# Which token blocks take the dense pass: the 4th, 5th and 8th in place of the 5th, 7th and 8th

## The chip, the cores and the metric

The kernel runs on one core of a Trainium2 chip. The metric is the device time of one execution in microseconds (us). The engines are named as the profile names them: PE (matrix products; PEld is its weight load), DVE (vector), ACT (scalar), POOL (GpSimd) and SP, whose queue issues most transfers.

## What is computed

One decoder layer over 1024 tokens of width 1024, in float32: a token mixer (stick-breaking attention and an mLSTM on one input projection, gated and projected), a layer norm, and then a mixture with 16384 experts, whose part matters here. Each of 8 heads picks 16 experts per token by the best sums of two sets of 128 keys:

```python
s1 = jnp.einsum('bshd,nd->bshn', q[..., 0, :], k1)
s2 = jnp.einsum('bshd,nd->bshn', q[..., 1, :], k2)
v1, i1 = lax.top_k(s1, 16); v2, i2 = lax.top_k(s2, 16)
...
top_s, pos = lax.top_k(cand, 16)
gates = jax.nn.softmax(top_s, axis=-1)
...
ue = jnp.take(u_tab, ib, axis=0)
act = jax.nn.gelu(jnp.einsum('btd,bthkd->bthk', hb, ue), approximate=False)
ve = jnp.take(v_tab, ib, axis=0)
return jnp.einsum('bthk,bthkd->btd', gb * act, ve)
```

The result of a token is this sum, plus a gated term of a per-layer embedding and the residual, through a last layer norm.

## The kernel before

The 1024 tokens are eight blocks of 128, worked on in three groups (`BLOCKS`): the 1st and 2nd; the 3rd, 4th and 5th; the 6th, 7th and 8th. The code counts blocks from 0, the text from 1. Each group goes through input projections, attention beside the mLSTM, branch projections, `keys` (the query projection and each head's best 16 keys), then `choose` (the best 16 sums and their experts, nearly all on DVE) beside `embed` (the rest of the layer's sum) and the next group's `project`.

A block's experts are worked out in one of two ways.

**Gathered.** Five blocks. `Experts` takes 128 rows of the table u and 128 rows of the table v (one for each of a token's 128 choices). POOL issues one indirect transfer for each row (`row`, L1079: 128 x 1024 floats into one of six buffers `vr`), and DVE multiplies and sums it: `vr<-vr,h1r` for u, `acc<-vr,w,acc` for v, both recorded at L139. The u rows of one block run alternately with the v rows of the block before it. Blocks are taken in the order in which they are chosen. This work lies in the background, between all else, from the first choice to the end.

**Dense.** Three blocks (`DENSE`). `dense` runs at the end over the whole tables in 128 pieces ("experts" in the loop over `e`): PE multiplies the tokens (`h1s`, 384 columns) with a piece of u (L276 to L278, into `m`), ACT applies gelu, DVE multiplies with the gates (`y<-y,gp`, L1043), and PE multiplies with the piece of v (L1019), accumulated in PSUM tiles `g` and `z`. There are two buffers `m`, so PE can be one piece ahead.

The gates come from a table in DRAM, `Gd`, which `spread` makes for each dense block, right after the block's `choose`. It transposes the choices (L965 to L967), and then works on 32 groups of four tokens. Of each group DVE makes one tile `ohA` (L977, 128 x 512), four one-hot rows `ohB` of 128 x 128 are made by the engines that `HOTS` names with a letter for each token (P is POOL, A is ACT with two instructions, D is DVE; L985 for P and D, L161 for A), PE multiplies (L987, four matmuls, into `z`, of which there are two), and ACT copies the product to `stage` (L173). After every four groups two transfers write `stage` to `Gd`. `ohA` and `ohB` come from one ring of `NCS` buffers (`csel`), and `stage` from the ring `c4` of four, which the attention's `kt` and `vt` use as well.

`ORDER` gives the order of the choices in the first two groups. In the third the dense blocks are chosen (and their tables made) beside `embed`, and the others beside the dense pass:

```python
h1s = halve()
yield from keys(o)
ex.rate = RATES["last"]
yield from Merge(choose(o, [t for t in o.tbs if t in DENSE]), embed(o))
ex.rate = RATES["dense"]
yield from Merge(choose(o, [t for t in o.tbs if t not in DENSE]), dense(h1s))
```

The order of the instructions on each engine is fixed when the program is built, by a scheduler that starts from this order of issue; each engine then runs its list in that order. The new names are `slot` (where a block's transposed tokens lie in `h1Ts`, by `OFF` and `SLOTS`) and `iota128`, the row that one-hot rows are compared with.

Of the kernel before, what the change touches and what calls it, by code (L numbers as in the profile page):

```python
# [20 lines left out]
P = 128  # L21
# [12 lines left out]
ORDER = [(0, 1), (2, 4, 3)]  # L34
# [3 lines left out]
NCS = 5  # L38
# [5 lines left out]
def _classes():  # L44
    """Where the n-th best of a head's sums can lie, n in fours: blocks of equal width, (to, from, a, b) each."""
    r, to = [], 0
    for lo in range(0, 16, 4):
        blocks = []
        for a0 in range(lo + 4):
            b0, b1 = lo // (a0 + 1), (lo + 4) // (a0 + 1)  # L50
            if b0 == b1:
                continue
            of, first, _, nb = [x for x in RANKS if x[1] <= a0 < x[2]][0]
            if blocks and blocks[-1][3] == a0 and blocks[-1][4:6] == (b0, b1) and blocks[-1][6] == (nb, first):
                blocks[-1] = blocks[-1][:3] + (a0 + 1,) + blocks[-1][4:]
            else:
                blocks.append((to, of + (a0 - first) * nb + b0, a0, a0 + 1, b0, b1, (nb, first)))
            to += b1 - b0
        r.append((blocks, to))
    return r  # L60
# [6 lines left out]
DENSE = (6, 7, 4)  # L67
OFF = (0, 128, 0)
HOTS = ("PAAD", "PAAD")
# [3 lines left out]
SLOTS = 4  # L73
# [7 lines left out]
class Merge:  # L81
    """Steps several emitters, always the one whose clock is furthest back."""
# [18 lines left out]
class Stream:  # L101
    """Streams the pieces of the weights in the order of their use, the loads and splits running ahead."""
# [17 lines left out]
def body(ctx: ExitStack, tc: tile.TileContext, a, out):  # L120
# [10 lines left out]
    class Chain:  # L131
        """The vector engine for work in the background, at most so many instructions in its queue at a time."""
# [15 lines left out]
    class Act:  # L148
        """The scalar engine: what needs one table set issues between two loads of sets."""
# [16 lines left out]
        def loose(self, o, i, f):  # L166
            """Out of that order: the set of the others is loaded again behind it."""
            x = nc.scalar.activation(o, i, f)
            if self.table not in (None, TABLES[f]):
                order(nc.scalar.preload_act_table_set(self.table), x)  # L170
# [100 lines left out]
    def mm(o, l, r, first, last):  # L271
        """One pass of plain float32 operands, or three of operands split in two."""
        if len(l) == 1:
            pe.matmul(o, l[0], r[0], start=first, stop=last)  # L274
        else:
            pe.matmul(o, l[0], r[0], start=first, stop=False)  # L276
            pe.matmul(o, l[0], r[1], start=False, stop=False)  # L277
            pe.matmul(o, l[1], r[0], start=False, stop=last)  # L278

    class Plain:  # L280
        """Operands of four slices each."""
# [12 lines left out]
    class Halves:  # L294
        """Two blocks of tokens, split in two."""
# [11 lines left out]
    def gemm(unit, other, blocks, evac, wide, width):  # L307
        """wide: the streamed weights are the moving operand, out = other^T @ w; else out = w^T @ other."""
# [29 lines left out]
    def standard(xt, st, read=None):  # L338
        """To mean 0 and variance 1, on the scalar engine; the sums of the halves may have been taken already."""
# [12 lines left out]
        # 1/sqrt by way of the logarithm, and a Newton step  # L352
# [10 lines left out]
    def layer_norm(xs, g, b):  # L363
        """In place, for as many blocks of tokens at a time as are given; one step for each."""
# [10 lines left out]
        # 1/sqrt: a first guess from the bits, good to 6%, then Newton steps to full precision  # L375
# [44 lines left out]
    # the order in which the weights are streamed  # L420
# [57 lines left out]
    def project(o):  # L478
        w, t0, hT = o.w, o.t0, o.hT
        rh = hT  # L480
        # gates of the recurrence, as rows
# [252 lines left out]
    def back(acc, hT, n, u, by, alone=False):  # L734
        """Adds a block's tokens, taken from their transposes, times the given diagonal."""
# [4 lines left out]
    def gates(o):  # L740
        """The attention's gates, but for the sigmoid."""
# [68 lines left out]
    def keys(o):  # L810
        w = o.w
        r1 = o.h1
        # the very first experts are wanted soon: the other block of tokens keeps its scores until they are chosen
# [59 lines left out]
    def choose(o, tbs):  # L873
        for tb in tbs:
# [48 lines left out]
            # a sum's place, in steps, plus its expert: the nearest to the place of the one that was taken  # L923
# [30 lines left out]
    def spread(tb, vidx, gt):  # L954
        """The gates of a block's tokens over all experts, to DRAM: per token a product of one-hot rows."""
# [7 lines left out]
        by = HOTS[tb in BLOCKS[-1]]  # L963
# [8 lines left out]
        for q in range(8):  # L972
            st = [c4("stage", (P, 64, 16)) for _ in range(2)]
            for t in range(q * 16, q * 16 + 16, 4):
# [4 lines left out]
                for k in range(4):  # L979
                    i2, gate, minus = (sel[:, i, t + k:t + k + 1] for i in (1, 2, 3))  # L980
                    if by[k] == "A":
                        act.activation(B[:, k], iota128, AF.Abs, bias=i2, scale=-1.0)
                        act.activation(B[:, k], B[:, k], AF.Relu, bias=gate, scale=minus)
                    else:
                        (pool if by[k] == "P" else vec).tensor_scalar(B[:, k], iota128, i2, gate, op0=OP.is_equal, op1=OP.mult)  # L985
# [14 lines left out]
    def halve():  # L1000
        """The dense blocks' tokens, split in two."""
# [7 lines left out]
    def dense(h1s):  # L1009
        """All experts' scores, times the gates, times the table v, accumulated in PSUM."""  # L1010
# [52 lines left out]
    class Experts:  # L1063
# [7 lines left out]
        def add(self, tb):  # L1071
            """For each block of tokens once its experts are chosen, and once the rest of its sum is stored."""
# [47 lines left out]
        def step(self):  # L1120
            """One slot; its time, or None when there is nothing to do."""
# [117 lines left out]
```

## Time and profile before

| | us |
|---|---|
| median of 3 runs (lowest to highest) | 3391.44 (3391.26 to 3399.57) |
| span of the profiled execution, first to last instruction | 3395.4 |
| PE busy | 3016.1 (89%) |
| DVE busy | 2652.0 (78%) |
| POOL busy | 1704.5 (50%) |
| ACT busy | 1108.9 (33%) |

The profile is of one execution. It shows its span, and no time outside it. Busy time is the time in which an engine has an instruction running; the chain that ended last follows the last instruction back through what released each step. The rows on which the prediction rests stand below, by view.

### The profile page before, as it was taken

How to read it: one execution, taken by the hardware profiler on the slowest of the kernel's cores; microseconds unless marked ns; L12 is line 12 of the kernel's file. 1: busy time of each engine (PE TensorE's matmuls, PEld its weight loads, DVE VectorE, ACT ScalarE, POOL GpSimd, SP SyncE). 2: the span in 40 equal slices, each digit the busy share in tenths (PEclk: the TensorE clock that was granted, in tenths of full speed). 3: DMA queues.
4: the chain of work that ended last, by engine and by line, in shares of the span. 5: the costliest groups of instructions: out<-in, count | busy, mean ns of one | idle time of the engine just before them, and what ended most of it. 6: DMA issues, size and time to landing. Idle time of an engine off the chain costs nothing.

```text
span 3395.4 us, 39154 instructions
## 1 busy us (share of the span) xinstructions
PE 3016.1 (89%) x12105; PEld 2024.1 (60%) x12105; DVE 2652.0 (78%) x5565; ACT 1108.9 (33%) x2561; POOL 1704.5 (50%) x1409
## 2 busy tenths in 40 slices
PE   7997999969899749998989664799999999999995
PEld 6876554555554535566555453566666666666663
DVE  5645998798699789888889977867777777776778
ACT  4626234521612445464141354411121111111110
POOL 0000255566533866646654577745545555544554
PEclk9898998969999859998999755799999999999997
DMA  6343798889989878977998776999999999999996
GB/s 212 130 155 136 246 351 324 318 276 378 357 307 319 323 267 308 339 263 251 376 358 320 272 266 229 311 344 351 354 361 349 345 348 350 350 353 357 352 343 244
DMA packets 341826, 1035.22 MB, mean 305 GB/s; under 512 B 38512, under 2 KB 95216, under 8 KB 341616
## 3 DMA queue, kind: packets, MB, share of 16 engines
q0 software_dynamic: 184320, 671.17, 55.2%
q1 hardware_dynamic: 157296, 361.55, 29.4%
q8 instruction: 96, 1.57, 0.2%
q14 instruction: 114, 0.93, 0.1%
HBM read 991.17 MB, written 41.42 MB: 304 GB/s over the span
## 4 chain that ended last, share of the span: by engine, by line
PE 69%; DVE 12%; issue 7%; POOL 5%; ACT 4%; DMA 2%; SPq 0%; DVEq 0%; POOLq 0%; ACTq 0%
PE g L274 17%; PE g L1019 13%; PE z L1019 6%; PE m L278 5%; PE m L276 5%; PE m L277 5%; PE g L784 3%; POOL ohB L985 3%; PE m L622 3%; POOL vr L1079 2%; PE z L987 2%; DVE vr L139 2%; PE z L583 2%; PE g L278 2%; PE g L276 2%
## 5 line engine op out<-in xcount | busy, mean ns | idle before, releaser
L1079 POOL DMA_INDIRECT vr<-in_u_dram,vidx x640 | 765.5, 1196 | 996.5 <-DVE V L139 385.8
L1079 POOL DMA_INDIRECT vr<-in_v_dram,vidx x640 | 793.2, 1239 | 648.5 <-DVE acc L139 333.9
L139 DVE SCALAR_TENSOR_TENSOR acc<-vr,w,acc 128x1024 f32<-128x1024 f32 x640 | 820.3, 1282 | 50.1 <-DMA vr<-in_v_dram,vidx 40.7
L139 DVE SCALAR_TENSOR_TENSOR vr<-vr,h1r 128x1024 f32<-128x1024 f32 x640 | 779.4, 1218 | 49.3 <-DMA vr<-in_u_dram,vidx 37.4
L1019 PE MATMUL g<-wf,y 128*128 128x512 f32 x1024 | 460.6, 592 | 1.6 <-DVE y L1043 1.6
L251 DVE TENSOR_TENSOR hl<-wf,hl 128x512 fp32r<-128x512 f32 x256 | 179.0, 699 | 306.3 <-PE m L277 268.7
L161 ACT ACTIVATE hl<-wf 128x512 fp32r<-128x512 f32 x256 | 160.5, 628 | 767.6 <-PE m L278 590.1
L276 PE MATMUL m<-h1s,hl 128*128 128x384 f32 x1024 | 395.3, 386 | 4.8 <-ACT y L161 3.1
L274 PE MATMUL g<-hT,wf 128*128 128x384 f32 x1024 | 344.1, 491 | 4.8 <-DVE gs L851 3.2
L278 PE MATMUL m<-h1s,hl 128*128 128x384 f32 x1024 | 345.8, 338 | 1.5 <-DVE hl L251 1.5
L277 PE MATMUL m<-h1s,hl 128*128 128x384 f32 x1024 | 345.4, 337 | 0.0
L1019 PEld LDWEIGHTS g<-wf,y 128*128 128x128 f32 x1024 | 192.2, 189 | 186.6 <-issue 169.7
L274 PEld LDWEIGHTS g<-hT,wf 128*128 128x128 f32 x1024 | 192.0, 191 | 135.1 <-issue 8.4
L987 PE MATMUL z<-ohA,ohB 128*128 128x128 f32 x768 | 182.7, 410 | 99.8 <-POOL ohB L985 90.5
L1019 PE MATMUL z<-wf,y 128*128 128x512 f32 x512 | 240.6, 592 | 0.0
L987 PEld LDWEIGHTS z<-ohA,ohB 128*128 128x128 f32 x768 | 155.7, 299 | 128.8 <-POOL ohB L985 115.4
L276 PEld LDWEIGHTS m<-h1s,hl 128*128 128x128 f32 x1024 | 193.8, 189 | 35.5 <-issue 31.3
L277 PEld LDWEIGHTS m<-h1s,hl 128*128 128x128 f32 x1024 | 193.8, 189 | 29.9 <-issue 29.9
L278 PEld LDWEIGHTS m<-h1s,hl 128*128 128x128 f32 x1024 | 193.4, 189 | 2.1 <-DVE hl L251 1.8
L274 PE MATMUL g<-h1T,wf 128*128 128x384 f32 x512 | 172.3, 491 | 0.1
L1019 PEld LDWEIGHTS z<-wf,y 128*128 128x128 f32 x512 | 97.3, 190 | 122.5 <-issue 122.2
L622 PE MATMUL m<-awT,vt 128*64 128x128 f32 x992 | 149.9, 302 | 18.7 <-ACT awT L173 12.1
(333 smaller groups left out, 4544.2 us busy)
## 6 DMA issues: line engine op xcount, KB each, us to landing
wf<-in_uE_dram SPq DMA_DIRECT2D x128, 512.0 KB
wf<-in_v_dram SPq DMA_DIRECT2D x128, 512.0 KB
wf<-in_wmain_dram SPq DMA_DIRECT2D x84, 512.0 KB
wf<-in_wgate_dram SPq DMA_DIRECT2D x48, 512.0 KB
wf<-in_wq_dram SPq DMA_DIRECT2D x48, 512.0 KB
Gd<-stage SPq DMA_DIRECT2D x48, 512.0 KB
gp<-Gd SPq DMA_DIRECT2D x32, 768.0 KB
wf<-in_wout_dram SPq DMA_DIRECT2D x24, 512.0 KB
```

What stands on the lines that cost most here:

```text
L139: x = getattr(vec, op)(*args, **kw)
L161: x = nc.scalar.activation(o, i, f, **kw)
L251: vec.tensor_tensor(lo, src, hi, op=OP.subtract)
L274: pe.matmul(o, l[0], r[0], start=first, stop=last)
L276: pe.matmul(o, l[0], r[0], start=first, stop=False)
L277: pe.matmul(o, l[0], r[1], start=False, stop=False)
L278: pe.matmul(o, l[1], r[0], start=False, stop=last)
L622: pe.matmul(po[rows, :P], vt[:, lo + s, row["e"] * 64:(row["e"] + 1) * 64], wT[:, s * P:(s + 1) * P], start=i == 0, stop=i == row["nb"] - 1)
L784: pe.matmul(acc, yT[k // 4][:, k % 4, n * P:(n + 1) * P], wo[u][k // 2][:, k % 2, :], start=k == 0, stop=k == 7)
L987: pe.matmul(pg[:, k], B[:, k], A[:, k], start=True, stop=True)
L1019: pe.matmul(acc[d][c], y[:, d * P:(d + 1) * P], wv[:, c * 512:(c + 1) * 512], start=e == 0, stop=e == P - 1)
L1079: pool.indirect_dma_start(out=vr, out_offset=None, in_=use[0], in_offset=bass.IndirectOffsetOnAxis(ap=idx[:, s:s + 1], axis=0))
```

## The change

The dense blocks become the 4th, 5th and 8th; gathered are the 1st, 2nd, 3rd, 6th and 7th. The second group chooses in the order 3rd, 4th, 5th, so that the tables of the 4th and 5th are made in that group's last stage, and the third group has one table to make and two choices beside the dense pass. POOL makes no one-hot rows: of each four, two are DVE's. The ring `csel` has 7 buffers for 5, there is room for five blocks of transposed tokens, since the 4th and the 5th must outlast the third group's writes, and the program is built with `dynamic_dma_scratch_size=8192`, which was not given before. Docstrings and comments went; the line numbers are the same.

```diff
-ORDER = [(0, 1), (2, 4, 3)]
+ORDER = [(0, 1), (2, 3, 4)]
...
-NCS = 5
+NCS = 7
...
-DENSE = (6, 7, 4)
-OFF = (0, 128, 0)
-HOTS = ("PAAD", "PAAD")
+DENSE = (3, 4, 7)
+OFF = (0, 256, 0)
+HOTS = "DAAD"
...
-SLOTS = 4
+SLOTS = 5
...
-        by = HOTS[tb in BLOCKS[-1]]
+        by = HOTS
...
-                        (pool if by[k] == "P" else vec).tensor_scalar(B[:, k], iota128, i2, gate, op0=OP.is_equal, op1=OP.mult)
+                        vec.tensor_scalar(B[:, k], iota128, i2, gate, op0=OP.is_equal, op1=OP.mult)
...
-    nc = bacc.Bacc("TRN2", target_bir_lowering=False, num_devices=1)
+    nc = bacc.Bacc("TRN2", target_bir_lowering=False, num_devices=1, dynamic_dma_scratch_size=8192)
```

How the lists of the engines change is shown at three places.

PE, from the second group's last projections (L274) to the first product of the third group's attention (L583); a piece of the difference, - is before:

```order
-L274 MATMUL g<-hT,wf 128x384 x4
+L274 MATMUL g<-hT,wf 128x384 x9
+L987 MATMUL z<-ohA,ohB 128x128 x8
+L274 MATMUL g<-hT,wf 128x384 x7
 L987 MATMUL z<-ohA,ohB 128x128 x104
+L965 MATMUL z<-ident,self 128x128
+L966 MATMUL z<-ident,self 128x128
+L967 MATMUL z<-ident,gt 128x128
+L987 MATMUL z<-ohA,ohB 128x128 x128
 L583 MATMUL z<-kt,qT 128x256
```

Of a table's 128 products 24 stand between projections, before as after; 104 follow the last of them, and now the whole table of the 5th block too, all ahead of the attention. In the third group one of two tables has gone from PE's list in the same way.

DVE, at the start of the dense pass of the changed kernel, between the gate products (L1043) of the third piece and those of the fourth; a cut from the middle of it:

```order
L1043 TENSOR_TENSOR y<-y,gp 128x192
L139 TENSOR_TENSOR ci<-top 128x8 x3
L139 TENSOR_TENSOR ci<-top 128x8x2
L251 TENSOR_TENSOR hl<-wf,hl 128x512
L139 CAST top<-pos 128x128
L139 TENSOR_TENSOR ci<-top 128x8x4
L139 SCALAR_TENSOR_TENSOR acc<-vr,w,acc 128x1024
L139 TENSOR_TENSOR ci<-top 128x8x2
L139 TENSOR_SCALAR top<-top 128x128
```

The `ci`, `top` and `pos` are the choice of the 6th block, and that of the 7th follows. Before the fourth piece's gate products stand 12 gathered rows of v and the end of one choice with the start of the next. From the last table's last `ohA` to the gate products of the seventh piece DVE's list holds 28 gathered rows and nearly two choices; before it held 21 and one.

DVE at the end, from the last piece's gate products to the statistics of the last layer norm, before:

```order
L1043 TENSOR_TENSOR y<-y,gp 128x192 x2
L139 SCALAR_TENSOR_TENSOR acc<-vr,w,acc 128x1024 x4
L1056 TENSOR_TENSOR accd<-accd,g 128x512 x2
L139 SCALAR_TENSOR_TENSOR acc<-vr,w,acc 128x1024
L1056 TENSOR_TENSOR accd<-accd,g 128x512 x2
L1056 TENSOR_TENSOR accd<-accd,z 128x512
L139 SCALAR_TENSOR_TENSOR acc<-vr,w,acc 128x1024
L1056 TENSOR_TENSOR accd<-accd,z 128x512
L139 SCALAR_TENSOR_TENSOR acc<-vr,w,acc 128x1024 x12
L370 BN_STATS st<-acc 128x6 x2
```

And of the change:

```order
L1043 TENSOR_TENSOR y<-y,gp 128x192 x2
L139 SCALAR_TENSOR_TENSOR acc<-vr,w,acc 128x1024 x4
L1056 TENSOR_TENSOR accd<-accd,g 128x512 x2
L139 SCALAR_TENSOR_TENSOR acc<-vr,w,acc 128x1024
L1056 TENSOR_TENSOR accd<-accd,g 128x512 x2
L139 SCALAR_TENSOR_TENSOR acc<-vr,w,acc 128x1024
L1056 TENSOR_TENSOR accd<-accd,z 128x512 x2
L139 SCALAR_TENSOR_TENSOR acc<-vr,w,acc 128x1024 x43
L370 BN_STATS st<-acc 128x6 x2
```

Behind the last gate products 18 gathered rows stood before, and now 49. Of the 1280 gathered rows 503 stood behind the first gate product of the dense pass, and now 544.

## Rows read from the trace of the kernel before

**Rows 1.** The page: chain that ended last, share of the span by engine.
```profile
PE 69%; DVE 12%; issue 7%; POOL 5%; ACT 4%; DMA 2%; SPq 0%; DVEq 0%; POOLq 0%; ACTq 0%
```

**Rows 2.** Busy time by stretch: length, busy us (instructions), granted clock, DMA share, GB/s.
```profile
1120.00:1226.00 106.00, 74.41 (x322) 58.07 (x320) 78.94 (x130) 60.87 (x185) 93.16 (x71) 0.77 0.83 294
1226.00:1257.00 31.00, 0.34 (x2) 0.34 (x2) 30.97 (x133) 5.12 (x7) 13.29 (x12) 0.50 0.81 283
1257.00:1925.00 668.00, 608.29 (x2405) 370.08 (x2404) 599.80 (x1279) 264.98 (x582) 373.29 (x311) 0.93 0.87 313
1925.00:2026.00 101.00, 66.59 (x259) 55.58 (x259) 71.02 (x128) 64.45 (x195) 86.53 (x65) 0.55 0.72 242
2026.00:2069.00 43.00, 0.88 (x3) 0.51 (x3) 42.48 (x141) 6.07 (x13) 25.48 (x20) 0.50 0.74 252
2069.00:2163.00 94.00, 63.93 (x259) 54.91 (x260) 65.67 (x118) 62.32 (x186) 81.60 (x62) 0.57 0.75 251
2163.00:3345.00 1182.00, 1177.28 (x4540) 813.26 (x4539) 859.34 (x1323) 211.21 (x383) 618.58 (x486) 1.00 0.96 349
```

**Rows 3.** PE in order of time, 5th block's table: start, us, what, [idle before].
```profile
1124.20 1.95 PE L987 MATMUL z<-ohA,ohB 128*128 128x128 f32 x16
...
1222.28 3.75 PE L987 MATMUL z<-ohA,ohB 128*128 128x128 f32 x16 [1.75 <-issue]
1256.69 1.19 PE L583 MATMUL z<-kt,qT 64*128 64x256 f32 x2 [30.66 <-DMA kt<-kTd]
```

**Rows 4.** PE in order of time, the tables of the 7th and 8th blocks.
```profile
1925.76 0.47 PE L965 MATMUL z<-ident,self 128*128 128x128 f32 x1 [7.20 <-DVE self L962]
...
1930.42 3.92 PE L987 MATMUL z<-ohA,ohB 128*128 128x128 f32 x16 [3.76 <-POOL ohB L985]
...
2024.04 1.09 PE L987 MATMUL z<-ohA,ohB 128*128 128x128 f32 x6 [0.34 <-ACT ohB L161]
2062.74 0.45 PE L965 MATMUL z<-ident,self 128*128 128x128 f32 x1 [37.61 <-DVE self L962]
...
2069.24 5.27 PE L987 MATMUL z<-ohA,ohB 128*128 128x128 f32 x24 [5.62 <-POOL ohB L985]
...
2160.39 2.08 PE L987 MATMUL z<-ohA,ohB 128*128 128x128 f32 x8 [2.00 <-POOL ohB L985]
```

**Rows 5.** Groups of instructions from 1925 to 2163 us: busy, mean ns, idle before.
```profile
L987 PE MATMUL z<-ohA,ohB 128*128 128x128 f32 x512 | 129.1, 427 | 68.2 <-POOL ohB L985 61.9 <-ACT ohB L161 5.5 <-ACT stage L173 0.4
...
L985 POOL TENSOR_SCALAR ohB<-iota,sel 128x128 f32<-128x128 f32 x64 | 97.5, 1524 | 15.0 <-PE z L987 12.8 <-issue 0.6 <-POOL ohB L985 0.2
...
L1079 POOL DMA_INDIRECT vr<-in_u_dram,vidx x41 | 49.1, 1197 | 14.5 <-issue 4.7 <-DVE top L139 2.6 <-DVE ci L139 1.7
...
L977 DVE TENSOR_TENSOR ohA<-iota,sel 128x512 f32<-128x512 f32 x64 | 43.8, 685 | 0.0
```

**Rows 6.** The same view over the whole span.
```profile
L1079 POOL DMA_INDIRECT vr<-in_u_dram,vidx x640 | 765.5, 1196 | 996.5 <-DVE V L139 385.8 <-DVE vr L139 283.0 <-issue 94.3
...
L985 DVE TENSOR_SCALAR ohB<-iota,sel 128x128 f32<-128x128 f32 x96 | 35.5, 370 | 74.9 <-PE z L987 72.5 <-issue 2.0
```

**Rows 7.** ACT in order of time, two groups of four tokens of the 8th block.
```profile
2123.19 0.66 ACT L173 ACTIVATE stage<-z 128x256 f32<-128x256 f32 x2 [1.73 <-PE z L987]
...
2125.59 1.64 ACT L161 ACTIVATE ohB<-ohB,sel 128x128 f32<-128x128 f32 x4
```

**Rows 8.** DVE in order of time: gate products of the sixth and seventh pieces.
```profile
2208.48 0.62 DVE L1043 TENSOR_TENSOR y<-y,gp 128x192 f32<-128x192 f32 x2
...
2216.68 0.63 DVE L1043 TENSOR_TENSOR y<-y,gp 128x192 f32<-128x192 f32 x2
```

**Rows 9.** DVE in order of time, from the last gate products to the end.
```profile
3343.98 0.62 DVE L1043 TENSOR_TENSOR y<-y,gp 128x192 f32<-128x192 f32 x2
3344.60 1.28 DVE L139 SCALAR_TENSOR_TENSOR acc<-vr,w,acc 128x1024 f32<-128x1024 f32 x1
...
3352.60 1.28 DVE L1056 TENSOR_TENSOR accd<-accd,g 128x512 f32<-128x512 f32 x2
...
3373.38 1.29 DVE L370 BATCH_NORM_STATS2 st<-acc 128x6 f32<-128x512 f32 x2
...
3387.26 3.67 DVE L387 SCALAR_TENSOR_TENSOR accd<-accd,rs,ln2b 128x1024 f32<-128x1024 f32 x3
```

## Prediction

> **What bounds the kernel now.** I read the chain of waits first: PE has 69% of it, DVE 12%, POOL 5% [rows 1]. So most of the time is PE's own work, which the change leaves alone: the same three blocks' worth of dense pass, the same projections. Then busy time by stretch [rows 2]. In the dense pass PE is busy for 1177.3 of 1182 us; nothing but PE counts there. In the three stretches in which a gate table is made PE's busy share falls to about two thirds at a granted clock of 0.55 to 0.77, and in the two in which a block is chosen with nothing beside it (1226 to 1257, 2026 to 2069) PE does next to nothing and DVE is busy throughout. These are the stretches that the change moves and shortens. In the tables POOL is busy for 87 of 101 and 82 of 94 us. The groups of instructions there say who is waited for: of PE's 68.2 us of idle time before L987, 61.9 ended with POOL's one-hot row, of 1524 ns each [rows 5]. So a table is bound by POOL, which makes one row of each four tokens between the gathers that it issues as well (1197 ns each).
>
> All sums are made against the profiled execution, whose span is 3395.4 us. No time around it is shown; it lies 4.0 us above the median of the three runs and within their range, so I take the difference off the median.
>
> **A group of four tokens.** Before, the 7th block's table took from 1930.42 to 2025.13 us, 94.7 us or 2.96 us for each of 32 groups; the 8th's took from 2069.24 to 2162.47, 2.91 [rows 4]. Without POOL, three engines are left:
> - ACT's work per group is unchanged: two groups ran from 2123.19 to 2127.23, 2.02 us each [rows 7].
> - PE: the first 24 records of the 8th's table are three groups (a product has two records: 512 records for 256 products), 5.27 us back to back at the lower clock, 1.76 each [rows 4].
> - DVE: one `ohA`, 0.685 us [rows 5], and now two `ohB` of 0.37 [rows 6], so 1.43, and with the gathered rows that its list holds between them. A row is 1.28 us [rows 9]. In the changed tables of the 5th and 8th blocks the list has about one row for two groups: 1.43 + 0.64 = 2.07. In the 4th's it has 30 for 32 groups.
>
> The unknown is how well these three interleave. The floor is ACT's 2.02, the ceiling 2.96, where nothing would be gained. I take **2.15**, near the floor, since two more one-hot buffers let DVE and ACT run further ahead of PE than before. A table is then 69 us.
>
> **The last stage of the second group (term A).** The 5th block's table began at 1124.20 and ended at 1226.03, 101.8 us, with the last projections between its first 24 products [rows 3]. The 4th block's takes its place. DVE's list is 32 x 1.43 + 30 x 1.28 = 84 us; as durations of neighbours overlap a little I take 80: -22. Behind it one choice and the attention followed: 1226.03 to 1256.69, 30.7 us. Now PE's list has the choice of the 5th, its table, and only then the attention. A choice up to the transposes it feeds took 2025.13 to 2062.74, 37.6 us [rows 4]; from the transposes to the first product 6.5 (2062.74 to 2069.24); the table 69; and `kt`, which waited last for its transfer at 1256.69 [rows 3], now gets its buffer from the table's last `stage` tiles: 2. That is 115.1 for 30.7, +84. **A = +62.** Only the 24 products stand beside projections; the second table is exposed.
>
> **The last stage of the third group (term B).** From the 7th block's transposes to the last product of the 8th's table: 1925.76 to 2162.47, 236.7 us [rows 4]. One choice and one table leave it. Left are 4.7 us from transposes to first product (1925.76 to 1930.42) and 69. **B = -163.**
>
> **The start of the dense pass (term C).** Two choices, not one, now stand beside the first pieces. From the last `ohA` to the seventh piece's gate products DVE's list has 7 rows more (9.0 us) and nearly one choice. A choice's own work is the 37.6 us less the 16 rows that its list holds (20.5): 17.1. So DVE is 26 us later at that point. Before, those products began at 2216.68, 8.2 us after the sixth's [rows 8], and the pace from there to the last, at 3343.98 [rows 9], is 9.32 us a piece over 121 pieces, PE's. PE can be one piece ahead, which covers about 9. **C = +17**, between 0 (two pieces ahead) and +33 (12 rows and one choice before the fourth piece's products, nothing covered).
>
> **The end (term D).** 49 rows instead of 18 stand behind the last gate products. Before, these 18 rows and six additions of 0.64 us took from 3344.60 to 3373.38; 24.9 us for 18 rows, 1.38 each [rows 9]. No PE work hides this. 31 x 1.38: **D = +43**. Bounds: 1.28, DVE alone (40), and the 2.43 of the dense pass, 1182 us for 486 rows with the tables' transfers beside them (75); the tail itself is the nearest.
>
> **At nothing.** Attention, branches and keys of the third group hold as many gathered rows as before to within two. POOL has 96 one-hot rows less, 142 us of work; outside the tables it waited mostly for DVE, for choices or for a buffer [rows 6], so this buys nothing by itself. The setting of `dynamic_dma_scratch_size` bears on POOL's transfers, and no row shows how: should it double the time that POOL lost to issue, 94.3 us for 640 gathers [rows 6], 0.15 each, the 49 last rows would cost 7 us more. The copies of the residual move from the 4th block to the 7th, two on ACT, which has 60% of that stage idle.
>
> **Sum.** 62 - 163 + 17 + 43 = **-41 us**; 3391.4 - 41 = **3350 us**.
>
> One rule of the skill speaks against the change. In the stretch 1925 to 2163 us POOL's gather took 1197 ns beside 64 one-hot rows of DVE, against 1196 over the whole span [rows 5, 6]: no hold is seen. The Trainium skill (SBUF — State Buffer, "Who interferes with whom") states that VectorE and GpSimd share a pair of ports, that VectorE's `tensor_scalar` may take both of it, and that the other then waits for the whole instruction, descriptor writing included. The trace's equal means don't bear that out for these operands. What it would cost is the third rival.
>
> **Rivals.**
> 1. *DVE takes POOL's place, slower than before.* DVE runs its list in order; a gathered row that is late holds the `ohA` and `ohB` behind it. If groups stay at 2.96 us, the three tables lose 22 + 2 x 26 = 74 us of what I gave them: +33, 3424 us. It decides from 2.60 us a group. For it: the 4th's DVE list alone is 84 us, and DVE was busy for 79 of 106 us there [rows 2]. Against it: PE waited for POOL, not DVE, and POOL now issues gathers without one-hot rows between them.
> 2. *The dense pass starts badly.* The two choices are chains of small instructions; if nothing is covered and the second choice holds the pieces behind as well (another 7 rows and 10 us), C is 52: -6, 3385 us, no change.
> 3. *The added one-hot rows hold the gathers.* 96 of them on DVE at 0.37 us, each holding one gather for its whole time and each seen on the path: +36, so -5, 3386 us, no change.
> 4. *Better than forecast.* Groups at ACT's 2.02, the 4th's table at 70, nothing lost at the start: -41 - 8 - 10 - 17 = -76, 3315 us.
>
> **How the numbers follow.** The forecast gets 0.65, the rivals 0.13, 0.11, 0.03 and 0.08. About 0.3% (10 us) is what a measurement of this kernel can tell from no change. Faster: the forecast, the fourth rival and a part of the second, 0.77. Same: most of the second and the third, 0.10. Slower: the first, 0.13. The forecast's own bounds are 8 us either way for the two tables, 10 for the 4th's, 17 for C, and 3 below to 15 above for D. The range reaches up over the second and third rivals to the edge of no change and down nearly to the fourth: 3318 to 3395.
>
> **What would show it.** Three tables of 65 to 75, 65 to 75 and 75 to 90 us between first and last L987; the third attention's first L583 at 1310 to 1330 us; the dense pass ending about 85 us earlier than 3344; 49 gathered rows behind it at 1.3 to 1.5 us. A group of more than 2.6 us, or PE idle for more than 40 us in the first seven pieces, makes the prediction wrong.

## The result, and the profile after

| | before | after |
|---|---|---|
| median of the runs, us (lowest to highest) | 3393.18 (3391.26 to 3399.57) | 3335.38 (3332.23 to 3338.68) |
| span of the profiled execution, us | 3395.4 | 3335.1 |
| DVE busy, us | 2652.0 | 2668.9 |
| POOL busy, us | 1704.5 | 1562.8 |

The change is faster: the ratio of the times is 0.9826, 95% interval 0.981 to 0.9842, or 58 us (1.7%). The forecast was 41 us.

The chain that ended last, as in [rows 1]: POOL has nearly left it, PE has a little less, DVE and ACT more.

```profile
PE 67%; DVE 16%; issue 8%; ACT 6%; DMA 2%; POOL 1%; SPq 0%; DVEq 0%; POOLq 0%; ACTq 0%
```

Busy time by stretch, as in [rows 2]: length, busy us (instructions) of PE, PEld, DVE, ACT and POOL, granted clock, DMA share, GB/s. The stretches are the 4th block's table, the choice behind it, the 5th's table, the middle of the third group, the 8th's table, and the dense pass with the first rows behind it.

```profile
1120.00:1197.00 77.00, 57.58 (x306) 46.78 (x306) 73.73 (x150) 57.24 (x180) 42.55 (x33) 0.89 0.94 345
1197.00:1242.00 45.00, 1.02 (x4) 0.68 (x5) 43.86 (x152) 8.76 (x20) 22.40 (x18) 0.52 0.73 247
1242.00:1301.00 59.00, 47.53 (x256) 36.72 (x256) 58.93 (x124) 57.44 (x183) 19.65 (x18) 0.96 0.87 296
1307.00:1975.00 668.00, 609.82 (x2405) 371.95 (x2405) 593.03 (x1231) 268.89 (x585) 366.27 (x307) 0.93 0.88 315
1975.00:2044.00 69.00, 54.71 (x283) 43.51 (x284) 68.86 (x164) 63.46 (x197) 24.70 (x25) 0.91 0.87 295
2044.00:3257.00 1213.00, 1184.37 (x4537) 813.13 (x4535) 898.51 (x1505) 210.84 (x384) 636.52 (x502) 0.99 0.96 348
```

A table now takes 58 to 76 us instead of 93 to 102. POOL has stopped being the busy engine in it; ACT (57.44 of 59) and DVE (58.93 of 59) are both full. The granted clock in the tables is 0.89 to 0.96 for 0.55 to 0.77, nearly the upper of its two levels; PE's idle time before L987, over all three tables, fell from 99.8 to 47.1 us.

PE in order of time through the last stage of the second group and the last of the third, answering [rows 3, 4]: start, us, what, idle before.

```profile
1120.24 2.33 PE L987 MATMUL z<-ohA,ohB 128*128 128x128 f32 x16 [0.98 <-DVE ohB L985]
...
1195.55 1.13 PE L987 MATMUL z<-ohA,ohB 128*128 128x128 f32 x8 [0.25 <-DVE ohB L985]
...
1237.11 0.45 PE L965 MATMUL z<-ident,self 128*128 128x128 f32 x1 [40.43 <-DVE rs L376]
...
1241.85 1.41 PE L987 MATMUL z<-ohA,ohB 128*128 128x128 f32 x5 [3.87 <-DVE ohB L985]
...
1298.14 2.02 PE L987 MATMUL z<-ohA,ohB 128*128 128x128 f32 x12 [0.19 <-ACT ohB L161]
1306.75 1.19 PE L583 MATMUL z<-kt,qT 64*128 64x256 f32 x2 [6.60 <-DMA kt<-kTd]
...
1975.17 0.47 PE L965 MATMUL z<-ident,self 128*128 128x128 f32 x1 [5.51 <-DVE self L962]
...
1978.54 1.86 PE L987 MATMUL z<-ohA,ohB 128*128 128x128 f32 x7 [2.47 <-DVE ohB L985]
...
2035.13 1.02 PE L987 MATMUL z<-ohA,ohB 128*128 128x128 f32 x6 [0.19 <-ACT ohB L161]
```

The three tables take 76.4, 58.3 and 57.6 us. (The last three products of the third stand a little later, between products of the first dense piece.) In steady state PE waits twice in each group, 0.19 us each time, mostly for ACT. ACT in the same table, one group and the start of the next, answering [rows 7]:

```profile
1269.54 0.73 ACT L173 ACTIVATE stage<-z 128x256 f32<-128x256 f32 x2
1270.07 0.50 ACT L161 ACTIVATE ohB<-iota,sel 128x128 f32<-128x128 f32 x1
1270.36 0.59 ACT L161 ACTIVATE ohB<-ohB,sel 128x128 f32<-128x128 f32 x1
1270.74 0.50 ACT L161 ACTIVATE ohB<-iota,sel 128x128 f32<-128x128 f32 x1
1271.04 0.59 ACT L161 ACTIVATE ohB<-ohB,sel 128x128 f32<-128x128 f32 x1
1271.42 0.74 ACT L173 ACTIVATE stage<-z 128x256 f32<-128x256 f32 x2
```

No row here has idle time before it. From `stage` to `stage` it is 1.88 us, the group's time; each row starts about 0.2 us before the one ahead of it has ended.

POOL's gathers and DVE's one-hot rows, groups over the whole span, answering [rows 6]:

```profile
L1079 POOL DMA_INDIRECT vr<-in_v_dram,vidx x640 | 786.1, 1228 | 729.6 <-DVE acc L139 271.2 <-issue 90.9 <-DVE y L1043 70.2
L1079 POOL DMA_INDIRECT vr<-in_u_dram,vidx x640 | 772.9, 1208 | 1013.1 <-DVE V L139 384.5 <-DVE vr L139 313.4 <-issue 93.1
...
L985 DVE TENSOR_SCALAR ohB<-iota,sel 128x128 f32<-128x128 f32 x192 | 57.5, 339 | 0.0
```

The 96 rows more cost DVE 22 us of busy time (57.5 for 35.5), for the 142 that POOL spent on as many. A gather of u takes 1208 ns for 1196.

DVE from the last gate products to the end, answering [rows 9]:

```profile
3238.97 0.62 DVE L1043 TENSOR_TENSOR y<-y,gp 128x192 f32<-128x192 f32 x2
...
3312.76 1.29 DVE L370 BATCH_NORM_STATS2 st<-acc 128x6 f32<-128x512 f32 x2
```

The dense pass ends 105.0 us earlier than before, and the rows behind it take 73.2 us instead of 28.8.

### The profile page after: what moved, and what is told of

The parts are those of the page before. It is cut to its first block, busy times and chain, and to the rows that moved or that the text cites. A ratio compares the mean times of both kernels' runs of the same rounds, so it can differ in the third digit from the quotient of the medians.

```text
span 3335.1 us, 38987 instructions
## 1 busy us (share of the span) xinstructions
PE 2974.0 (89%) x12105; PEld 1982.6 (59%) x12105; DVE 2668.9 (80%) x5661; ACT 1101.9 (33%) x2560; POOL 1562.8 (47%) x1313
## 4 chain that ended last, share of the span: by engine, by line
PE 67%; DVE 16%; issue 8%; ACT 6%; DMA 2%; POOL 1%; SPq 0%; DVEq 0%; POOLq 0%; ACTq 0%
PE g L274 15%; PE g L1019 13%; PE z L1019 6%; PE m L278 5%; PE m L276 5%; PE m L277 5%; PE g L784 3%; DVE acc L139 3%; PE m L622 3%; ACT ohB L161 2%; PE z L583 2%; DVE vr L139 2%; PE g L276 2%; PE g L278 2%; PE g L277 2%
## 5 line engine op out<-in xcount | busy, mean ns | idle before, releaser
L1079 POOL DMA_INDIRECT vr<-in_u_dram,vidx x640 | 772.9, 1208 | 1013.1 <-DVE V L139 384.5
L1019 PE MATMUL g<-wf,y 128*128 128x512 f32 x1024 | 462.8, 594 | 14.7 <-DVE y L1043 14.7
L274 PE MATMUL g<-hT,wf 128*128 128x384 f32 x1024 | 342.7, 489 | 5.8 <-DVE gs L851 3.2
L1019 PEld LDWEIGHTS g<-wf,y 128*128 128x128 f32 x1024 | 193.1, 190 | 201.9 <-issue 171.3
L274 PEld LDWEIGHTS g<-hT,wf 128*128 128x128 f32 x1024 | 191.7, 191 | 136.1 <-issue 7.7
L1019 PE MATMUL z<-wf,y 128*128 128x512 f32 x512 | 240.6, 592 | 0.0
L987 PE MATMUL z<-ohA,ohB 128*128 128x128 f32 x768 | 137.9, 320 | 47.1 <-ACT ohB L161 18.7
L274 PE MATMUL g<-h1T,wf 128*128 128x384 f32 x512 | 173.1, 493 | 1.5 <-ACT h1T L161 1.4
L1019 PEld LDWEIGHTS z<-wf,y 128*128 128x128 f32 x512 | 97.3, 190 | 122.5 <-issue 122.2
L987 PEld LDWEIGHTS z<-ohA,ohB 128*128 128x128 f32 x768 | 112.1, 210 | 74.5 <-ACT ohB L161 53.1
```

Source lines behind the costliest of these rows:

```text
L987: pe.matmul(pg[:, k], B[:, k], A[:, k], start=True, stop=True)
L1019: pe.matmul(acc[d][c], y[:, d * P:(d + 1) * P], wv[:, c * 512:(c + 1) * 512], start=e == 0, stop=e == P - 1)
L1079: pool.indirect_dma_start(out=vr, out_offset=None, in_=use[0], in_offset=bass.IndirectOffsetOnAxis(ap=idx[:, s:s + 1], axis=0))
```

## The experiments

The theory was the prediction's: a table was long because POOL made one of four one-hot rows between its gathers, and with that gone the rest is bookkeeping (a stage gains a table, another loses one, the end gets more rows). The rival was that the places of the tables bring the gain. The first four runs take the change apart, on one chip.

**POOL's rows alone.** From before:

```diff
-HOTS = ("PAAD", "PAAD")
+HOTS = ("DAAD", "DAAD")
```

> The kernel before, with POOL's one-hot rows given to DVE and nothing else (blocks 5, 7, 8 stay dense, ring of 5). Theory (a table is as long as it is because POOL makes one row of four between its gathers): the three tables shorten as they did in the change, by 22 to 25 us for the 5th's and 26 to 35 each for the other two, -74 to -95; eight more rows stand behind the last gate products in DVE's list (26 for 18), 1.4 each, +11. Sum -63 to -84: 3310 to 3330 us. Rival 1 (the gain of the change comes from where the tables stand, and DVE holds the groups without POOL as POOL did): the tables stay at 90 to 100 us and the time within 10 us of 3391, or above it for the 8 rows.

Measured: 3334.95 us, ratio 0.9819 (0.9797 to 0.9841). The theory's range missed by 5 us; the rival falls. Two characters give what the whole change gives. The tables took 80.9, 66.2 and 66.3 us.

**All but the blocks.** As above, with `NCS = 7` and the scratch setting.

> The kernel before with all of the change but the blocks: POOL's one-hot rows on DVE, ring of 7, dynamic_dma_scratch_size=8192; blocks 5, 7 and 8 stay dense. Theory: tables at the change's 76, 58 and 58 us for 101.8, 94.7 and 93.2, -97; 41 rows behind the last gate products for 18, 23 x 1.4, +33. Sum -64: about 3330 us, so the move of the blocks is worth nothing beyond 10 us. Rival 1 (the move is the gain): within 10 us of 3391.

Measured: 3339.52 us, 0.9837 (0.9819 to 0.9854). The tables took 73.8, 58.7 and 61.9 us, so the two buffers are worth 4 to 8 us in each. (Part of this is that the lists now hold 31, 17 and 17 gathered rows within the tables for 34, 21 and 21.) The dense pass ended at 3255.82 for 3276.14 with the ring of 5, and all of those 20 us were given back: 41 rows behind the last gate products took 61.4 us, where 26 had taken 39.6.

**The blocks with POOL's rows.** From the change:

```diff
-HOTS = "DAAD"
+HOTS = "PAAD"
...
-                        vec.tensor_scalar(B[:, k], iota128, i2, gate, op0=OP.is_equal, op1=OP.mult)
+                        (pool if by[k] == "P" else vec).tensor_scalar(B[:, k], iota128, i2, gate, op0=OP.is_equal, op1=OP.mult)
```

> The changed kernel with POOL's one-hot rows put back (one of each four tokens), blocks 4, 5 and 8, ring of 7 and the scratch setting kept. Theory: groups go back to 2.9 to 3.0 us, the 4th's table by 25, the 5th's and 8th's by 34 each, +93; 37 rows behind the last gate products for 49, 12 x 1.42, -17. Sum +76: about 3411 us, slower than the kernel before. Rival 1 (the move is the gain): 3335 to 3350 us.

Measured: 3362.32 us, 0.9905 (0.9888 to 0.9921). Both fail. POOL's rows came back and the tables took 92.7, 74.6 and 75.5 us, not 92 to 101. (As in the change, the last three products of the third stand later, between products of the first dense piece; with them it is 81.4.) Something else in the change had made POOL's tables shorter.

**The ring.** From the change, `NCS = 5`.

> The changed kernel with the ring of one-hot tiles at 5 buffers for 7. The prediction put groups at 2.15 us because of the two more buffers; the change measured 1.89. If the buffers made the difference, the groups go to 2.15 or more, +8 for each of three tables; 40 rows stand behind the last gate products for 49, -13: together about 3347 us with tables of 67 us or more. If the ring does not matter, the tables stay at 58 and the 9 rows are the only difference: 3322 us.

Measured: 3346.32 us, 0.9868 (0.985 to 0.9886), as in the first case. The tables took 85.8, 65.4 and 63.6 us.

That made the ring the suspect for the third run, and a second theory: with a ring of 5, in which a group takes two buffers, POOL can't work ahead.

**The ring alone.** From before, POOL's rows kept:

```diff
-NCS = 5
+NCS = 7
...
-    nc = bacc.Bacc("TRN2", target_bir_lowering=False, num_devices=1)
+    nc = bacc.Bacc("TRN2", target_bir_lowering=False, num_devices=1, dynamic_dma_scratch_size=8192)
```

> The kernel before with the ring of one-hot tiles at 7 buffers and the scratch setting, POOL's rows and the blocks as before. With the blocks moved, POOL's rows and a ring of 7, tables took 92.7, 74.6 and 81.4 us, not the 95 and 2.96 a group that the theory said. Theory 2 (POOL was late because a ring of 5 let it start a group's row only when PE had finished an earlier group; with 7 it works ahead between gathers): tables of about 92, 78 and 78 here, -10 -17 -15, ten more rows behind the last gate products (28 for 18) at 1.4, +14. Sum -28: about 3367 us. Rival 2 (the gain of that run came from the blocks' places, the ring is nothing): tables of 100, 95 and 93, 3395 to 3409 us.

Measured: 3364.55 us, 0.9903 (0.9887 to 0.992), tables of 92.4, 75.1 and 82.0 us. Theory 2 holds. POOL in order of time, two groups of the 7th block's table and the start of a third, in the kernel before:

```profile
1961.21 1.37 POOL L985 TENSOR_SCALAR ohB<-iota,sel 128x128 f32<-128x128 f32 x1 [0.71 <-PE z L987]
1962.75 1.45 POOL L1079 DMA_INDIRECT vr<-in_u_dram,vidx  x1 [0.17 <-issue]
1964.24 1.73 POOL L985 TENSOR_SCALAR ohB<-iota,sel 128x128 f32<-128x128 f32 x1
1966.14 1.02 POOL L1079 DMA_INDIRECT vr<-in_v_dram,vidx  x1 [0.17 <-issue]
1967.87 1.37 POOL L985 TENSOR_SCALAR ohB<-iota,sel 128x128 f32<-128x128 f32 x1 [0.71 <-PE z L987]
```

and with the ring of 7:

```profile
1963.33 0.94 POOL L985 TENSOR_SCALAR ohB<-iota,sel 128x128 f32<-128x128 f32 x1
1964.43 1.04 POOL L1079 DMA_INDIRECT vr<-in_v_dram,vidx  x1 [0.17 <-PE z L987]
1965.52 1.47 POOL L985 TENSOR_SCALAR ohB<-iota,sel 128x128 f32<-128x128 f32 x1
1967.16 1.11 POOL L1079 DMA_INDIRECT vr<-in_u_dram,vidx  x1 [0.17 <-ACT stage L173]
1968.31 0.93 POOL L985 TENSOR_SCALAR ohB<-iota,sel 128x128 f32<-128x128 f32 x1
```

Before, POOL waited for PE at every second one-hot row (PE's product had to free the buffer), and two groups took 6.66 us. With 7 buffers that wait is gone and the rows themselves are shorter, 1.47 and 0.93 us: two groups in 4.98. The wait isn't the whole of it. The two tables of the third group lost 31 us; 12.8 of these are POOL's waits for PE [rows 5], about 7 are shorter one-hot rows (means of 1.35 and 1.48 us for 1.55 and 1.50), and about 9 are gathers that no longer lie within them (52 for 60), some of which stand behind the dense pass now. So the change holds two cures for the same tables:

| us | POOL's rows kept | POOL's rows on DVE |
|---|---|---|
| blocks 5, 7, 8, ring 5 | 3393 to 3397 (before) | 3335 |
| blocks 5, 7, 8, ring 7 | 3365 | 3340 |
| blocks 4, 5, 8, ring 5 | not run | 3346 |
| blocks 4, 5, 8, ring 7 | 3362 | 3335 (the change) |

The ring alone gives 32 us, the rows alone 60; together they give no more than the rows alone. Moving the blocks is worth 2 and 4 us with a ring of 7, less than the intervals tell apart, and costs 11 with the ring of 5. The scratch setting was not run by itself; it came with the ring. In the gathers nothing of it is seen: those of u and v took 1181 and 1259 ns without it (POOL's rows alone), 1176 and 1257 with it (all but the blocks).

**The rows at the end.** In the change and the three runs above without POOL's one-hot rows the last gathered row ends between 3312 and 3319 us, though the dense pass ends anywhere from 3239 to 3277. So it was asked what a row behind the pass costs, and whether it is cheaper elsewhere. First, the change without 32 of them (the sums of the 7th block lack these terms):

```diff
-            for s in range(P):
+            for s in range(P - 32 * (tb == 6)):
                 self.row(vidx, s, (a["v"], lambda vr, s=s: evec.scalar_tensor_tensor(
```

> The changed kernel without the last 32 of the 6th... 7th block's gathered rows of v (the last block that is gathered; its output lacks 32 of 128 terms): 17 rows stand behind the last gate products for 49, all else in place. Term D (each of these rows costs 1.42 us of the end, nothing hides it): 32 x 1.42, -45: 3290 us. Rival (the end is set by transfers that run late anyway, or by the norm that waits for another block): less than 25 us gained, 3310 us or above.

Measured: 3290.76 us, 0.9688 (0.9671 to 0.9704). From the last gate products to the norm, DVE in order of time:

```profile
3235.48 0.62 DVE L1043 TENSOR_TENSOR y<-y,gp 128x192 f32<-128x192 f32 x2
...
3262.84 1.29 DVE L370 BATCH_NORM_STATS2 st<-acc 128x6 f32<-128x512 f32 x2
```

26.7 us for 73.2: 1.45 for each of the 32, all on the path. Then three kernels with `ED = 2` for 1, which lets the scheduler put two gathered rows together on DVE and so moves rows forward.

> The changed kernel with the depth of the chain of gathered rows on DVE at two for one (ED = 2), which lets the scheduler place rows closer together: 374 rows stand before the first table for 337, none in the last table for 17, and 34 behind the last gate products for 49. Theory D (a row that stands behind the last gate products costs 1.42 us, since POOL issues one in 1.42 and PE is done): -15 x 1.42 = -21, and the last table without its 17 rows at most 5 us shorter; against it up to 37 rows more, 1.28 each of DVE, lie in the first stages, where DVE was busy for 626 of 715 us and may hold PE. 3310 to 3320 us if those are covered. Rival (DVE's time is needed there, each of the 37 rows costs its 1.28 us): +47, 3360 us.

> Blocks 5, 7 and 8 dense as before, POOL's rows on DVE, ring of 7, ED = 2: no gathered row stands behind the last gate products (41 with ED = 1), 371 before the first table, 395 for 324 in the middle of the third group. Theory D: the 41 rows' 62 us at the end go, -55 or so after the additions and the norm that stay; 3280 to 3290 us if DVE's list in front has room for the rows. Rival (the rows cost PE as much where they stand now: transfers had 0.88 of the engines there and DVE 0.9 of its time): 3330 to 3345 us.

> The kernel before with ED = 2 alone: no row behind the last gate products for 18. Theory D: -25 us, 3370 us, tables unchanged to 4 us. Rival (rows cost as much in front): 3395 us or above.

Measured: 3379.41 us (0.9947, 0.993 to 0.9963), 3443.25 (1.013, 1.0113 to 1.0147) and 3502.88 (1.0311, 1.0294 to 1.0328). The first two are slower than even the rival said, and the third is 106 us above the kernel before, where the rival said no gain. In the first, PE begins the first table 55.4 us later than in the change, for 37 rows more before it, 1.50 each if all of the delay is put down to them:

```profile
1175.61 0.61 PE L987 MATMUL z<-ohA,ohB 128*128 128x128 f32 x4
```

In the second, by DVE's list, 871 rows stand before the first gate products for 749, and PE's first L1019 comes at 2230.58 us for 2077.77, 1.25 us for each by the same reckoning. The choice between the two tables alone takes 61.3 us for 38.4. Busy time in the dense pass of that kernel and, below, of the one with `ED = 1`:

```profile
2300.00:3398.00 1098.00, 1098.00 (x4247) 759.50 (x4246) 699.23 (x1025) 193.42 (x354) 473.24 (x378) 1.00 0.87 315
```

```profile
2078.00:3256.00 1178.00, 1173.44 (x4519) 808.73 (x4518) 861.48 (x1332) 211.05 (x383) 616.13 (x488) 1.00 0.96 351
```

With rows two deep the pace from the eighth piece on is the same (9.30 us a piece for 9.31), but DVE works 0.64 of it for 0.73, and the transfers' share is 0.87 for 0.96. So `ED = 2` did not only take the 41 rows from the end: it took 81 more out of the pass, where PE hides them, and put all 122 where DVE is what PE waits for. A row costs about 1.25 to 1.5 us in front, nothing in the pass, 1.45 behind it; and the pass holds some 490 in every version with `ED = 1` (484 to 496 by DVE's list).

**One more on DVE.** From the change, `HOTS = "DADD"`.

> The changed kernel with one of ACT's two one-hot rows of each group given to DVE too (DADD). In the change a group took 1.89 us, with ACT never idle and DVE hardly (57.4 and 58.9 of 59 us). If ACT sets a group, it shortens: ACT's part falls to about 1.2, DVE's list is 0.60 + 3 x 0.26 and 9 rows for 32 groups, 1.75, so tables of 56 us for 58 and 70 for 76, -10 in all; 69 rows for 49 stand behind the last gate products, +28. Sum +18: 3353 us. If DVE sets it, tables are no shorter or longer by 0.26 a group, 8 us each: +40, 3375 us.

Measured: 3354.5 us, 0.9874 (0.9857 to 0.989), as in the first case in total; of its parts the 5th's table did not follow. By stretch:

```profile
1242.00:1297.00 55.00, 38.52 (x237) 34.53 (x236) 55.00 (x142) 42.72 (x120) 10.42 (x11) 0.86 0.70 246
```

ACT is freed (42.72 of 55), DVE is full, and the table takes 58.7 us for 58.3; the 4th's takes 68.9 for 76.4 and the 8th's 54.9 for 57.6, each with seven gathered rows fewer in it. Which of the two full engines sets a group in the change is shown by the first run with `ED = 2`. Its table of the 8th block holds no gathered row, and takes 57.2 us all the same:

```profile
2066.58:2123.74 57.16, 45.65 (x252) 34.40 (x252) 38.72 (x112) 57.16 (x182) 0.00 (x0) 1.00 0.35 138
```

DVE has 18 us to spare there and ACT none. So ACT sets the group in the change, and the gathered rows only fill DVE's time beside it; DVE takes over at nearly the same length when it gets one of ACT's rows, so little can be won by moving it. The 69 rows behind the pass then cost what was expected.

**The second choice.** In the change PE's longest wait of the dense pass is this one, PE in order of time, and above it DVE's gate products that end it:

```profile
2094.67 0.61 DVE L1043 TENSOR_TENSOR y<-y,gp 128x192 f32<-128x192 f32 x2
```

```profile
2095.07 5.99 PE L1019 MATMUL g<-wf,y 128*128 128x512 f32 x8 [13.51 <-DVE y L1043]
```

Since the third piece's last, at 2059.99, DVE's list held 12 gathered rows and some 100 small instructions of the two choices. The edit lets the 7th block's choice begin eight pieces later:

```diff
+    def late(o, tbs):
+        for n, tb in enumerate(tbs):
+            if n:
+                for _ in range(8):
+                    yield 9.2
+            yield from choose(o, [tb])
...
-                yield from Merge(choose(o, [t for t in o.tbs if t not in DENSE]), dense(h1s))
+                yield from Merge(late(o, [t for t in o.tbs if t not in DENSE]), dense(h1s))
```

> The changed kernel, with the second of the two choices beside the dense pass held back by eight pieces. In the change 12 gathered rows and most of a choice stand before one piece's gate products in DVE's list, and PE stood idle 13.5 us for them. Theory C (two choices in a row are what the start of the dense pass lost): that idle time goes, the pass shortens from 1202.8 us by 13 to 20, and 55 rows stand behind the last gate products for 49, +8.5. Sum -5 to -12: 3323 to 3331 us. Rival (the start was late for other reasons, the pass from the first piece on is held by transfers): the pass stays at 1203, 3340 to 3345 us.

Measured: 3328.64 us, 0.9801 (0.9784 to 0.9817). Busy time in the first 70 us of the pass, in the change and, below, in this run:

```profile
2036.00:2106.00 70.00, 49.13 (x168) 32.44 (x167) 65.56 (x256) 15.77 (x27) 30.94 (x24) 0.83 0.83 279
```

```profile
2031.00:2101.00 70.00, 65.95 (x254) 44.96 (x255) 64.25 (x166) 16.96 (x31) 37.79 (x29) 1.00 0.95 339
```

PE is busy for 65.95 us instead of 49.13. From the last regular product of the table (2030.99) to the last gate products (3211.62) the pass takes 1180.6 us for the change's 1202.8; the 55 rows behind it take 82.5 for 73.2. With sixteen pieces:

> As the run with the second choice held back by eight pieces, but by sixteen; 55 rows stand behind the last gate products in both. Theory C (what the start lost was two choices in a row, wherever the second goes afterwards): the same dense pass of about 1181 us and the same time as with eight, 3320 to 3330 us. Rival (eight pieces gained by a lucky place among the transfers): the pass is back at 1190 us or more, 3335 us or above.

Measured: 3326.61 us, 0.9799 (0.9781 to 0.9816), a pass of 1181.2 us. Between these two places it makes no difference. These are the fastest kernels here that compute the whole layer, 7 to 9 us below the change in the median; they weren't timed against it directly, and the intervals of the ratios to before still overlap at their ends (0.981 is the lower end of the change).

## Why the prediction was right, point by point

The sign held, and each term went the way and by about the amount that was forecast; the sum was 19 us too cautious. Of the signs named beforehand the rows behind the pass came as said (49, at 1.42 us each) and the 4th's table did (76.4 us), and three were missed to the better side: two tables of 58 us where 65 to 75 were named, the third attention at 1306.75 us for 1310 to 1330, and a dense pass that ends 105 us earlier for about 85. All against the profiled execution:

| term | forecast | measured |
|---|---|---|
| A, second group's last stage | +62 | +50.1 |
| middle of the third group | 0 | -0.6 |
| B, third group's last stage | -163 | -175.7 |
| C, dense pass from the last table to its end | +17 | +21.3 |
| D, from the last gate products to the norm | +43 | +44.4 |
| norm and output | 0 | +0.4 |
| sum | -41 | -60.3 |

**The step that was mis-sized is the group of four tokens: 2.15 us forecast, 1.80 to 1.82 measured** over the tables of the 5th and 8th (58.3 and 57.6 us over 32). These two tables alone came 22 us under their forecast, and the other differences took 3 back. The floor of 2.02 was read from ACT's list [rows 7] from the first start to the last end of two groups, 4.04 us. That holds the end of the last row (0.10), which the next group's first row can overlap, and a short stop (0.16: the second `stage` starts 0.45 us after the row ahead of it, where rows of that kind start 0.29 apart). Without them it is 1.89 a group; in the change it is 1.88 from start to start, and 31 times that is 58.3 (the first group's rows were ready when the first product ran). What was called the floor lay above the floor. The reason given for coming near it, the two more buffers, is borne out: 65.4 and 63.6 us with five.

**Term A.** The 4th's table took 76.4 us for a forecast of 80, the choice behind it 40.4 for 37.6, from transposes to the first product 4.7 for 6.5, the second table 58.3 for 69, and `kt` 6.6 for 2. The last 4.0 lie before the stage: the first product came at 1120.24 for 1124.20 before. They can't be credited to the change: five other kernels whose lists of PE and DVE are the same up to there had it at 1118.60 to 1125.13.

**Term B.** 3.4 us from the transposes to the first product and 57.6 of table, for 4.7 and 69.

**Term C.** The mechanism and its size hold, and holding the second choice back takes all of it off again (1180.6 us against 1181.5 before). Forecast was a shortfall that grows up to the seventh piece; of the 20.9 us that PE stood idle in the first 70, one wait of 13.5 came at the fourth.

**Term D.** 49 rows in 73.2 us less six additions of 0.64 are 1.42 each; 1.38 was forecast. The prediction didn't say what sets that pace. POOL in the same stretch, in order of time, shows it:

```profile
3257.12 1.01 POOL L1079 DMA_INDIRECT vr<-in_v_dram,vidx  x1 [0.30 <-issue]
3258.43 1.02 POOL L1079 DMA_INDIRECT vr<-in_v_dram,vidx  x1 [0.30 <-issue]
...
3262.40 1.68 POOL L1079 DMA_INDIRECT vr<-in_v_dram,vidx  x1 [0.30 <-issue]
```

POOL issues without a stop, 0.30 us between one gather and the next; 37 of them begin between 3252.31 and 3305.03, one in 1.46 us, while DVE needs 1.28 for a row. Seven of the 37 take 1.47 to 1.86 us, and the trace says why. DVE beside the long one above:

```profile
3261.98 1.28 DVE L139 SCALAR_TENSOR_TENSOR acc<-vr,w,acc 128x1024 f32<-128x1024 f32 x1 [0.70 <-DMA vr<-in_v_dram,vidx]
```

The gather began 0.42 us into this row and ended at 3264.08, 0.82 us after the row did. Those of 1.02 began when the row beside them had 0.2 us left. The last section has this for all gathers.

**At nothing** held for the middle, and for the scratch setting as far as the gathers show it. Nor is a gain from POOL's 142 us seen outside the tables.

**The rivals.** The first (groups stay at 2.96) is out by the tables. The second (C = 52) saw the right place and over-priced it. The third: gathers took 1040 ns in the 8th's table and 1098 in the 5th's, for 1197 before, with twice as many one-hot rows of DVE beside them (in the 4th's 1326, for 1273 in the table that stood there before). More directly, the 42 gathers of the change that begin while DVE runs a one-hot row took 0.94 us in the median, as did the 182 that begin with DVE idle. So these rows hold nothing. The Trainium skill's rule that it rested on (SBUF — State Buffer, "Who interferes with whom", the part on VectorE's `tensor_scalar`) is not borne out for these operands here. The fourth, 3315, had the group right in kind, but at 2.02, and C = 0, which only the held-back choice gives.

**What the move of the blocks does by itself** the terms don't say; the run with all but the blocks does. From it to the change A is +79.7 us, the middle -6.0, B -104.6, C +19.0 and D +11.8. What is gained in front, 31 us, the start of the dense pass and the rows behind it take back. So the forecast came true by its group of four tokens, and not by the move that it spent most of its terms on.

**What the prediction did not see** is that its explanation for the gain was one of two. It read "PE waits for POOL's row" [rows 5] and took POOL's work for the price. Part of what PE waited for was POOL's own wait for a buffer: the 12.8 us `<-PE z L987` stand in the same rows, and with two more buffers the two tables of the third group lost 31 us. Part, again, was POOL being held by DVE's gathered rows (last section). The forecast didn't depend on either, because the change takes POOL out of the groups; a forecast for the ring alone would have been wrong by 30 us.

## What to carry to other kernels

When PE waits for an engine's row, look at what that engine's row waits for: a ring that is too small looks like a slow engine. Work that fills gaps (here the gathered rows) is worth its place: shortening the stretch that hid it sends it to the end of the kernel at full price, and pulling it forward charges it to the engine that is scarce there, so count it in every stretch before pricing a gain. And two exposed chains in a row are worth separating: holding the second choice back by eight pieces gave back all that the start of the dense pass had lost.

## What was not expected of the hardware

POOL's one-hot row has no fixed price. The rows in the two tables before, min, median and max in ns:

```profile
L985 POOL TENSOR_SCALAR ohB<-iota,sel x64: 780/1371/2486, 1929.0 to 2159.5; 128x128 f32<-128x128 f32 x64
```

POOL in the 5th's table of the kernel with the moved blocks and POOL's rows, in order of time, and below it DVE:

```profile
1273.36 2.27 POOL L985 TENSOR_SCALAR ohB<-iota,sel 128x128 f32<-128x128 f32 x1
...
1279.10 0.80 POOL L985 TENSOR_SCALAR ohB<-iota,sel 128x128 f32<-128x128 f32 x1
```

```profile
1273.77 1.28 DVE L139 SCALAR_TENSOR_TENSOR acc<-vr,w,acc 128x1024 f32<-128x1024 f32 x1
...
1277.48 0.68 DVE L977 TENSOR_TENSOR ohA<-iota,sel 128x512 f32<-128x512 f32 x1
1280.01 0.35 DVE L985 TENSOR_SCALAR ohB<-iota,sel 128x128 f32<-128x128 f32 x1 [1.85 <-PE z L987]
```

The row that ran from 1279.10, with DVE idle until 1280.01, took 0.80 us. The one from 1273.36 had a gathered row of DVE inside it, 1.28 us, and took 2.27, 0.2 over the sum. The Trainium skill has a rule for this (SBUF — State Buffer, "Who interferes with whom"): a VectorE instruction with two inputs in SBUF contends with a GpSimd instruction that reads SBUF. The traces agree. Over the three runs with POOL's rows and `ED = 1`, 38 rows ran beside neither a gathered row nor an `ohA` of DVE (two inputs each), and took 0.78 to 0.90 us; 64 had at least 1.2 us of a gathered row beside them, and took 1.72 to 2.76. Spans on POOL are rough, and no run took the gathered rows away to test it alone.

The gathers are held in the same way. In the change, the 182 that begin with DVE idle took 0.94 us, none more than 0.95. The 591 that begin inside a gathered row of DVE took 1.40 on average, and where that row had more than 0.3 us left (334), the gather ended 0.81 us after the row, in nine of ten cases to within 0.05. The 43 that begin inside `art<-z,asp`, the same operation of DVE with its input `z` in PSUM, took 0.94 again. So the 1197 ns of a gather in the tables before [rows 5] are not its own price: about a quarter of a microsecond of them is this hold, and the pace of 1.46 us behind the dense pass is 0.94, 0.30 between gathers, and 0.2 of this hold.
